# A two-layer hybrid decoder trunk: normalisations without GpSimd products, a power and one Newton step for the root, a new order at the first stage and the layer boundary, and compression interleaved with projections

## The chip, the cores and the metric

The kernel runs on one core of a Trainium2 chip. The metric is the time of one execution in microseconds on the device. The engines are named as in the profile: PE is the matrix engine, with its weight loads listed apart as PEld, DVE the vector engine, ACT the scalar engine, POOL the GpSimd engine, and SP the queue that issues every DMA of this kernel. Each engine works through its own list of instructions in order.

## The reference

The input x has 512 tokens of 1024 float32 channels. Two layers follow one another, each of this form:

```python
h = rms_norm(x, norm_g[l])              # x * rsqrt(mean(x*x) + 1e-6) * g
proj = h @ w_in[l]                      # 1024 -> 4376
...
y_nsa = nsa_attention(q, k_c, v_c, k_s, v_s, k_w, v_w, gates, ...)   # three branches
y_lru = rg_lru(u_lru, ...)              # short convolution, two gates, linear scan
y_conv = conformer_conv(glu_a, glu_b, ...)   # GLU, 31 taps per channel, LayerNorm, 512x512
mixed = concat([y_nsa * silu(z_nsa), y_lru * silu(z_lru), y_conv * silu(z_conv)])
x = x + mixed @ w_out[l]                # 1536 -> 1024
```

A last rms_norm with final_g closes the trunk. In the attention, one branch works on compressed keys and values: blocks of 32 tokens (31 of them, 16 apart) go through a small two-layer network, `silu(blk @ w1) @ w2`, with a 2048 x 256 matrix w1, once for keys and once for values.

## The kernel before

Every float32 product of matrices is made of three matmuls on split operands: a number is cast to the shorter type of the matrix engine (hi), and the rest, number minus hi, is the low part (lo); hi·hi, hi·lo and lo·hi are summed. So each weight tile needs a cast on ACT (line 146) and a subtraction on DVE (line 149, `lower`). x is held as four blocks of 128 tokens, t = 0 to 3, and the normalised input h as H, transposed: channels on partitions, tokens along the row, hi and lo.

Buffers come from pools with tags. Tag p has ten buffers of 1024 elements per partition, tag t sixteen of 512, "raw" two for weights as loaded, whi and wlo three each for split weights. PSUM has three buffers of tag ps, two each of tr and acc, and one of po. A tile waits until an earlier tile of its tag is free. The order of an engine's instructions is set by a scheduler from the order in the program, except where the program fixes it (`manual_schedule`): ACT and DVE in the first stage by the string START, PE in the last rows of the attention by LAST_ROWS.

The stages of a layer, in program order:

1. Normalisation. For a block: sum of squares on ACT (lines 221 and 296), the reciprocal root on DVE (`rsqrt`, line 208: a first guess from the bits of the number and three Newton steps, seven instructions on one element per partition), and the product with root and gain g. In layer 0 two blocks have the whole product on DVE (`product`, line 302) or in two parts, x times g on POOL (line 306) and times the root on ACT (line 309). In layer 1 and at the end (`rms_norm`, line 227) x times g is on POOL (line 232) and times the root on ACT (line 239); for the block t = 0 one half is on DVE (line 237). The gain is loaded as a broadcast to all partitions, 512 KB (`load_g`).
2. `turned` (line 273): eight transposes of a block on PE, a cast on ACT (line 278) and a lower on DVE (line 279) make its part of H.
3. The value projection (line 333): for each block 24 matmuls with 280 columns. Its weights are split by `value_weights` in eight pieces of 280 columns (casts on ACT, subtractions on POOL, or in START's v steps on DVE), held in sixteen buffers of tag t. In both layers the blocks go in the order 3, 2, 1, 0.
4. Channel parameters (lines 347 to 358): small loads into a buffer of tag t, transposed on PE.
5. The other projections (line 204, `proj`): for each tile of 128 output channels 24 matmuls with 512 columns, in the order glu, q, k_c and v_c, k, u_lru, z_nsa, z_lru, z_conv. In layer 0 the tables for the rotation are computed ahead of them on DVE. Between them stand the 31-tap filter on DVE (line 387, 120 instructions a layer), the scan, and the compression: `do_prep(c)` builds its operands, `do_main(c)` (line 617) loads w1 in two halves, splits each into two tiles and makes 64 matmuls of 256 columns (line 631). Keys (c = 0) come after z_nsa, values (c = 1) after z_lru.
6. LayerNorm of the convolution (`do_ln`, which calls `rsqrt`), part of the output projection (line 429, added to x on line 431), the 512x512 matmul (line 719), and the attention (lines 780 to 830).
7. `last_rows`: the attention's block 0, woven by LAST_ROWS with the output projection of its own part. Steps r are the rows of x: r31 is block 3, half 1. The last ones are r21, r31, r11, r01, r00. The output weights of half 1 are split into four buffers of tag p ("ow").

In layer 1, stage 1 also writes x back to memory (line 318), to be loaded again for the output projection.

## Time and profile before

| what | value |
|---|---|
| median of 3 runs | 809.26 us (807.87 to 812.53) |
| the profiled execution's own time | 808.92 us |
| its span, first to last instruction | 807.2 us |
| mean granted clock of PE | 0.985 |
| ACT busy | 462.8 us |
| POOL busy, instructions | 121.0 us, 184 |
| loads and stores | 82.53 MB, 102 GB/s in the mean |

The page gives busy time per engine, the span in 40 slices of 20.2 us each (each digit the busy share of one slice in tenths), the chain of waits that ended last, and groups of instructions. "Waits" name the instruction that came last before an engine went on. A matmul's duration in the records covers its whole way through the array, so matmuls overlap: the time of a group is better read from its first to its last start.

### The profile page before, as it was taken

To read this page: it belongs to the slowest core of one execution; us is meant where nothing else is said; L and a number is where in the kernel's file an instruction comes from. 1 tells how busy PE (TensorE), PEld (TensorE's weight loads), DVE (VectorE), ACT (ScalarE), POOL (GpSimd) and SP (SyncE) were. 2 spreads that over 40 slices of the span, in tenths; PEclk is the share of its full clock that TensorE was granted. 3 is DMA by queue.
4 is the path that set the end of the run, shared out by engine and by line. 5 is a ranking of instruction groups with operands and counts; after the bars stand their busy time and mean duration, and the time that the engine had idled before them with its cause. 6 is when DMAs were issued, how large, how long until landed. Compare 5 with 4: busy or idle time off the path is not lost.

```text
span 807.2 us, 11053 instructions
## 1 busy us (share of the span) xinstructions
PE 756.8 (94%) x3812; PEld 609.9 (76%) x3812; DVE 692.9 (86%) x1308; ACT 462.8 (57%) x908; POOL 121.0 (15%) x184
## 2 busy tenths in 40 slices
PE   3899999998999999999889999999899999999992
PEld 3778888687788786887777888776787878778872
DVE  6679999999998888878783899999999878888867
ACT  5434577684446566765562247669543466676654
POOL 4000000000000134343610000000000003333324
PEclk9999999999999999999979999999999999999997
DMA  5522375717542200102422225771664140010002
GB/s 190 164 80 86 105 185 128 186 59 240 201 147 79 78 1 2 53 2 58 157 95 94 97 64 153 183 179 37 202 231 157 52 158 1 1 54 1 2 27 104
DMA packets 68387, 82.53 MB, mean 102 GB/s; under 512 B 6616, under 2 KB 56856, under 8 KB 68332
## 3 DMA queue, kind: packets, MB, share of 16 engines
q1 hardware_dynamic: 68332, 81.83, 33.0%
q8 instruction: 30, 0.49, 0.3%
q14 instruction: 25, 0.20, 0.1%
HBM read 68.19 MB, written 4.19 MB: 90 GB/s over the span
## 4 chain that ended last, share of the span: by engine, by line
PE 60%; DVE 25%; ACT 6%; issue 4%; DMA 3%; POOL 2%; SPq 0%; DVEq 0%; POOLq 0%; ACTq 0%
PE acc L204 29%; PE acc L429 11%; DVE cv L387 6%; PE po L814 4%; DVE wlo L149 4%; PE pt L799 3%; PE acc L719 3%; ACT P L788 2%; PE acc L333 2%; PE ps L780 2%; PE ps L781 2%; DVE nw L214 2%; DVE xc L506 2%; POOL P L792 1%; DVE ss L215 1%
## 5 line engine op out<-in xcount | busy, mean ns | idle before, releaser
L204 PE MATMUL acc<-H,whi 128*128 128x512 f32 x1024 | 327.1, 399 | 0.6 <-ACT whi L146 0.6
L204 PEld LDWEIGHTS acc<-H,whi 128*128 128x128 f32 x1024 | 192.7, 189 | 47.8 <-issue 3.1
L204 PE MATMUL acc<-H,wlo 128*128 128x512 f32 x512 | 204.4, 400 | 0.3 <-DVE wlo L149 0.3
L146 ACT CAST whi<-raw 128x1024 fp32r<-128x1024 f32 x100 | 104.7, 1049 | 167.4 <-PE acc L204 126.7
L792 POOL TENSOR_SCALAR P<-P,hm,gt 128x384 f32<-128x384 f32 (+3 forms) x128 | 80.8, 640 | 593.9 <-DVE hm L790 586.0
L387 DVE SCALAR_TENSOR_TENSOR cv<-sg,dww,cv 128x496 f32<-128x496 f32 (+27 forms) x240 | 167.4, 742 | 0.9
L149 DVE TENSOR_TENSOR wlo<-raw,whi 128x1024 fp32r<-128x1024 f32 x100 | 123.7, 1237 | 25.0 <-ACT whi L146 24.6
L204 PEld LDWEIGHTS acc<-H,wlo 128*128 128x128 f32 x512 | 96.8, 189 | 24.0 <-issue 1.2
L788 ACT ACTIVATE P<-ps,hm 128x384 f32<-128x384 f32 (+3 forms) x128 | 67.0, 531 | 19.2 <-DVE hm L785 17.4
L802 DVE TENSOR_TENSOR pt<-pt 128x512 fp32r<-128x512 f32 (+1 forms) x88 | 54.4, 638 | 12.4 <-ACT pt L801 11.4
L785 DVE TENSOR_REDUCE hm<-ps 128x1 f32<-128x384 f32 (+3 forms) x88 | 55.2, 634 | 8.5 <-PE ps L782 6.0
L801 ACT CAST pt<-pt 128x512 fp32r<-128x512 f32 (+1 forms) x88 | 45.9, 548 | 24.2 <-PE pt L799 20.2
L814 PE MATMUL po<-pt,vv 128*128 128x256 f32 (+1 forms) x304 | 56.7, 303 | 0.4
L814 PEld LDWEIGHTS po<-pt,vv 128*128 128x128 f32 x304 | 44.4, 189 | 9.4 <-ACT pt L801 4.5
L799 PE MATMUL pt<-ident,P 128*128 128x128 f32 x320 | 47.7, 275 | 1.3 <-POOL P L792 0.6
L780 PE MATMUL ps<-KH,QS 128*128 128x384 f32 (+3 forms) x128 | 44.8, 362 | 1.4 <-ACT P L788 1.2
L799 PEld LDWEIGHTS pt<-ident,P 128*128 128x128 f32 x320 | 37.0, 140 | 6.5 <-POOL P L792 3.9
L781 PE MATMUL ps<-KL,QS 128*128 128x384 f32 (+3 forms) x128 | 40.7, 329 | 0.0
L431 DVE TENSOR_TENSOR x<-x,acc 128x512 f32<-128x512 f32 x48 | 32.7, 681 | 1.7 <-PE acc L429 1.3
L333 PE MATMUL acc<-wvh,H 128*128 128x280 f32 x128 | 29.4, 323 | 1.7 <-ACT H L278 1.7
L395 ACT COPY rs<-ru 32x512 f32<-32x512 f32 x48 | 29.7, 619 | 0.8
L276 PE MATMUL pt<-ident,hnat 128*128 128x128 f32 x64 | 13.4, 360 | 17.1 <-DVE hnat L303 8.6
(238 smaller groups left out, 1281.0 us busy)
## 6 DMA issues: line engine op xcount, KB each, us to landing
raw<-in_w_in_dram SPq DMA_DIRECT2D x30, 1024.0 KB
raw<-in_w_out_dram SPq DMA_DIRECT2D x12, 1024.0 KB
raw<-in_cmp_w_dram SPq DMA_DIRECT2D x8, 1024.0 KB
x<-in_x_dram SPq DMA_DIRECT2D x8, 512.0 KB
raw<-in_w_in_dram SPq DMA_DIRECT2D x4, 512.0 KB
QS<-rs SPq DMA_DIRECT2D x8, 256.0 KB
QS<-ru SPq DMA_DIRECT2D x8, 256.0 KB
KH<-rs SPq DMA_DIRECT2D x8, 256.0 KB
```

The costliest lines, as they stand in the source:

```text
L146: S.copy(out, in_)
L149: (eng or V).tensor_tensor(out, in_, hi.bitcast(F32), op=OP.subtract)
L204: PE.matmul(p, w[k], h[k], start=n == 0, stop=n == 23)
L387: V.scalar_tensor_tensor(a[:, s:], u[:, :T - s], dww[:, ct, j:j + 1], a[:, s:], op0=OP.mult, op1=OP.add)
L429: PE.matmul(p, h[:, k], w, start=m == 0, stop=m == 11)
L780: PE.matmul(sc[:, r, :], q, KH[g][:, b, :L], start=r == 0, stop=False)
L781: PE.matmul(sc[:, r, :], q, KL[g][:, b, :L], start=False, stop=False)
L785: V.tensor_reduce(hm[:, 0, :nh], sc, axis=AX.X, op=OP.min)
L788: S.activation(P[:, r * L:(r + 1) * L], sc[:, r, :], AF.Exp, scale=-1.0, bias=hm[:, 0, r:r + 1], accum_out=hm[:, 1, r:r + 1])
L792: G.tensor_scalar(P[:, r * L:(r + 1) * L], P[:, r * L:(r + 1) * L], hm[:, 2, r:r + 1], GA[i][:, h0 + r, 1 + b:2 + b], op0=OP.mult, op1=OP. ...
L799: PE.transpose(pt[:, kb, :], P[:, kb * 128:(kb + 1) * 128], ident)
L814: PE.matmul(po, v, PT[w][:, kb].rearrange("p r q -> p (r q)"), start=False, stop=last and kb == i and w == 1)
```

## The change

Five things are changed.

The root: `rsqrt` takes four times the mean square and raises it to the power -0.5 on POOL, which gives half the root wanted, and makes one Newton step on DVE with three short instructions. All its callers pass 4 where they passed 0.5.

The products: none is left on POOL. `rms_norm` makes one DVE instruction of x, root and gain (two halves for t = 0).

The first stage: layer 0's gain is loaded as one row and spread over the partitions by two matmuls with a row of ones, into two PSUM buffers of tag ps, from which the products on DVE read. The value weights' load stands ahead of x's blocks 1 and 0. START is rewritten; products are by halves, and the value weights are split in three pieces (3, 3 and 2 rows of 128 channels), all lowers on DVE, into the buffers of KH, KL and QS instead of tag t.

The boundary: layer 1's value weights are split ahead of the normalisation, the blocks go in the order 2, 3, 1, 0 (also at the end), and only two of the four "ow" tiles are taken from tag p, the others from whi and wlo.

The compression: `do_main` is given a generator of projections and makes two projection tiles ahead of each half of w1; z_nsa is woven into the keys' compression and z_lru into the values'. The values' `do_prep` comes ahead of the keys' `do_main`.

```diff
-START = "q3 c3 p3 q2 g2 q1 c2 t30 t31 s2 w2 c1 q0 p1 w0 c0 w1 t20 w3 t21 p0 v4 t10 v7 t01 t00 v5 v6 t11"
+START = "q3 c3 p30 p31 q2 t30 c2 t31 p20 w0 p21 q1 t20 c1 w1 t21 p10 q0 p11 w2 t10 c0 t11 p00 p01 t00 t01"
...
+    G.memset(one, 1.0)
+    power = const.tile([128, 1], F32, name="power")
+    G.memset(power, -0.5)
...
-    def rsqrt(y, hv):
-        s = work.tile([128, 1], F32, name="nw", tag="nw", bufs=4)
-        V.tensor_scalar(y.bitcast(I32), hv.bitcast(I32), -0.5, float(0x5f3759df - 2 ** 22 - 2 ** 31), op0=OP.mult,
-                        op1=OP.add)
-        for _ in range(3):
-            V.scalar_tensor_tensor(s, y, hv, y, op0=OP.mult, op1=OP.mult)
-            V.scalar_tensor_tensor(y, s, 1.5, y, op0=OP.subtract, op1=OP.mult)
+    def rsqrt(y, v4):
+        s = work.tile([128, 2], F32, name="nw", tag="nw", bufs=4)
+        G.tensor_tensor(y, v4, power, op=OP.pow)
+        V.tensor_scalar(s[:, 0:1], v4, -1.0, None, op0=OP.mult)
+        V.scalar_tensor_tensor(s[:, 1:2], y, s[:, 0:1], y, op0=OP.mult, op1=OP.mult)
+        V.scalar_tensor_tensor(y, s[:, 1:2], 3.0, y, op0=OP.add, op1=OP.mult)
...
-    def rms_norm(x, gb, name, last=False):
-        y = pair(name)
-        ss = rms_sums(x, y)
-        for n in range(1 if last else 2):
-            G.tensor_tensor(y[:, n], x[:, n], gb[:, n], op=OP.mult)
...
+        for n in (slice(0, 1), slice(1, 2)) if halves else (slice(0, 2),):
+            V.scalar_tensor_tensor(y[:, n], x[:, n], ss[:, 2:3], gb[:, n], op0=OP.mult, op1=OP.mult)
         return y
...
         if l == 0:
-            load_x(0, X, (3,))
-        gb = load_g(norm_g[l])
+            grow = pair("grow")[0:1].rearrange("p a c -> p (a c)")
+            SP.dma_start(out=grow, in_=norm_g[0:1, :])
+            load_x(0, X, (3, 2))
+        else:
+            gb = load_g(norm_g[l])
+        wv = [w_cols(l, (COL["v_s"], 128), (COL["v_w"], 152), rows=rows) for rows in ((0, 6), (6, 2))]
         if l == 0:
-            load_x(0, X, (2, 1, 0))
-        wv = [w_cols(l, (COL["v_s"], 128), (COL["v_w"], 152), rows=(k, 4)) for k in (0, 4)]
+            load_x(0, X, (1, 0))
...
-        def value_weights(k, eng=G):
-            src = wv[k // 4][:, k % 4, :]
-            hi = big(f"wvh{k}", F32R)[:, :280]
-            lo = big(f"wvl{k}", F32R)[:, :280]
+        def value_weights(j):
+            n = 3 if j < 2 else 2
+            src = wv[j // 2][:, 3 * j % 6:3 * j % 6 + n, :]
+            hi, lo = (main.tile([128, 4 if j == 2 else 2, 512], F32R, name="wv",
+                                tag=(f"kh{j}", f"kl{j}")[w] if j < 2 else f"qs{w}", bufs=1) for w in range(2))
...
+            gp = [psum.tile([128, 512], F32, name="acc", tag="ps", bufs=3) for n in range(2)]
+            for n in range(2):
+                PE.matmul(gp[n], one, grow[:, n * 512:(n + 1) * 512], start=True, stop=True)
...
-            def product(t):
-                V.scalar_tensor_tensor(hs[t], X[t], ss[t][:, 2:3], gb, op0=OP.mult, op1=OP.mult)
-            def gained(t):
-                G.tensor_tensor(hs[t], X[t], gb, op=OP.mult)
-            def scale(t):
-                S.activation(hs[t], hs[t], AF.Copy, scale=ss[t][:, 2:3])
+            def product(t, n):
+                V.scalar_tensor_tensor(hs[t][:, n], X[t][:, n], ss[t][:, 2:3], gp[n], op0=OP.mult, op1=OP.mult)
...
         else:
-            for t in (3, 2, 1, 0):
+            for j in range(3):
+                value_weights(j)
+            for t in (2, 3, 1, 0):
                 SP.dma_start(out=saved[t], in_=X[t])
-                h = rms_norm(X[t], gb, "hnat", last=t == 0)
+                h = rms_norm(X[t], gb, "hnat", t == 0)
                 for n in range(2):
                     turned(t, h, n)
-            for k in range(8):
-                value_weights(k)
...
-        for t in (3, 2, 1, 0):
+        for t in (2, 3, 1, 0) if l else (3, 2, 1, 0):
...
-                hi, lo = w_split(r[:, k:k + 2], [pair("ow", F32R) for _ in range(2)] if pairs else None)
+                hi, lo = w_split(r[:, k:k + 2], [pair("ow", F32R) for _ in range(2)] if pairs and k else None)
...
-        def do_main(c):
+        def do_main(c, between):
...
             for hf in range(2):
+                for _ in range(2):
+                    next(between)
                 r = raw_tile().rearrange("p (k c) -> p k c", c=256)
...
-        do_z_nsa()
-        do_main(0)
+        do_prep(1)
+        do_main(0, z_nsa())
         do_scan()
-        do_prep(1)
-        do_z_lru()
-        do_main(1)
+        do_main(1, z_lru())
...
-    for t in (3, 2, 1, 0):
-        o = rms_norm(X[t], gb, "o", last=t == 0)
+    for t in (2, 3, 1, 0):
+        o = rms_norm(X[t], gb, "o", t == 0)
```

The generators `z_nsa` and `z_lru` are the former `do_z_nsa` and `do_z_lru` with a `yield` behind each tile. In LayerNorm only the factor 0.5 becomes 4.

More of the change, by code (lines that the diff above doesn't have):

```diff
@@ L75, in tile_hybrid_trunk @@
     identb = const.tile([128, 128], BF16, name="identb")
-    zeros = big("zeros")[:, :192]
+    zeros, one = (lambda z: (z[:, :192], z[0:1, 384:]))(big("zeros"))
     ones = const.tile([128, 1], F32, name="ones")
@@ L279, in turned @@
             V.tensor_tensor(H2[1][n][:, :, sl], p, H2[0][n][:, :, sl].bitcast(F32), op=OP.subtract)
-        def value_weights(k, eng=G):
-            src = wv[k // 4][:, k % 4, :]
-            hi = big(f"wvh{k}", F32R)[:, :280]
-            lo = big(f"wvl{k}", F32R)[:, :280]
+        def value_weights(j):
[3 more added lines that the diff above has]
+                                tag=(f"kh{j}", f"kl{j}")[w] if j < 2 else f"qs{w}", bufs=1) for w in range(2))
+            hi, lo = (w.rearrange("p a b -> p (a b)")[:, :n * 280].rearrange("p (k c) -> p k c", k=n) for w in (hi, lo))
             cast(hi, src)
-            lower(lo, src, hi, eng)
-            WV[k] = (hi, lo)
+            lower(lo, src, hi)
+            WV[3 * j:3 * j + n] = [(hi[:, k], lo[:, k]) for k in range(n)]
         if l == 0:
             hs, ss = {}, {}
+            gp = [psum.tile([128, 512], F32, name="acc", tag="ps", bufs=3) for n in range(2)]
+            for n in range(2):
+                PE.matmul(gp[n], one, grow[:, n * 512:(n + 1) * 512], start=True, stop=True)
             def squares(t):
@@ L298, in chain @@
             def chain(t):
-                V.tensor_scalar(ss[t][:, 3:4], ss[t][:, 0:1], 0.5 / DM, 0.5 * EPS, op0=OP.mult, op1=OP.add)
+                V.tensor_scalar(ss[t][:, 3:4], ss[t][:, 0:1], 4.0 / DM, 4.0 * EPS, op0=OP.mult, op1=OP.add)
                 rsqrt(ss[t][:, 2:3], ss[t][:, 3:4])
-            def product(t):
-                V.scalar_tensor_tensor(hs[t], X[t], ss[t][:, 2:3], gb, op0=OP.mult, op1=OP.mult)
-            def gained(t):
-                G.tensor_tensor(hs[t], X[t], gb, op=OP.mult)
-            def scale(t):
-                S.activation(hs[t], hs[t], AF.Copy, scale=ss[t][:, 2:3])
-            steps = dict(q=squares, c=chain, p=product, g=gained, s=scale, t=lambda t, n: turned(t, hs[t], n),
-                         w=value_weights, v=lambda k: value_weights(k, V))
+            def product(t, n):
+                V.scalar_tensor_tensor(hs[t][:, n], X[t][:, n], ss[t][:, 2:3], gp[n], op0=OP.mult, op1=OP.mult)
+            steps = dict(q=squares, c=chain, p=product, t=lambda t, n: turned(t, hs[t], n), w=value_weights)
             with tc.manual_schedule(engines={mybir.EngineType.Activation, mybir.EngineType.DVE}):
@@ L581, in do_z_lru @@
                 ML32.append(HL[ct])
+                yield
         def do_z_conv():
@@ L680, in do_ln @@
                 V.bn_aggr(mv[:, 0:2], st)
-                V.tensor_scalar(mv[:, 1:2], mv[:, 1:2], 0.5, 0.5 * EPS, op0=OP.mult, op1=OP.add)
+                V.tensor_scalar(mv[:, 1:2], mv[:, 1:2], 4.0, 4.0 * EPS, op0=OP.mult, op1=OP.add)
                 rsqrt(mv[:, 2:3], mv[:, 1:2])
```

19 lines of the change are left out of this document (7 added, 12 removed).

## The prediction

> **What bounds the kernel now.** I read the page first (busy shares and the 40 slices), then a table of stretches, then the timeline and the chain of waits at the three places where the table shows TensorE (PE) idle.
>
> ```profile
> span 807.2 us, 11053 instructions
> PE 756.8 (94%) x3812; PEld 609.9 (76%) x3812; DVE 692.9 (86%) x1308; ACT 462.8 (57%) x908; POOL 121.0 (15%) x184
> PE   3899999998999999999889999999899999999992
> ```
>
> PE is busy nearly everywhere, so 807.2 - 756.8 = 50.4 us of idle PE is about all that reordering can win, with time at a reduced clock added. The slices put most of it at the start, at the layer boundary (slices 20 and 21) and at the end.
>
> ```profile
> 0.00:30.00 30.00, 16.73 (x90) 14.44 (x91) 22.36 (x53) 16.55 (x31) 9.07 (x22) 1.00 0.55 174
> 36.40:38.90 2.50, 0.76 (x7) 0.40 (x6) 0.52 (x2) 0.59 (x2) 0.00 (x0) 1.00 0.06 22
> 38.90:44.00 5.10, 5.10 (x17) 4.05 (x17) 0.55 (x3) 0.46 (x1) 0.00 (x0) 0.67 0.22 53
> 135.00:240.00 105.00, 101.97 (x457) 79.28 (x457) 103.74 (x145) 60.12 (x85) 0.00 (x0) 1.00 0.53 162
> 401.60:405.20 3.60, 0.00 (x0) 0.00 (x0) 3.50 (x10) 1.14 (x2) 2.15 (x2) 0.96 0.01 2
> 405.20:415.30 10.10, 8.11 (x35) 7.42 (x36) 9.42 (x28) 6.50 (x14) 3.32 (x3) 0.51 0.13 52
> 427.90:429.80 1.90, 0.44 (x5) 0.40 (x5) 0.52 (x2) 0.38 (x2) 0.73 (x2) 1.00 0.05 20
> 525.00:630.00 105.00, 102.12 (x456) 79.41 (x456) 101.42 (x141) 61.35 (x86) 0.00 (x0) 1.00 0.51 157
> 792.70:807.20 14.50, 0.00 (x0) 0.00 (x0) 10.00 (x34) 6.11 (x10) 3.91 (x4) 0.66 0.37 145
> ```
>
> The columns are the stretch, its length, then busy time of PE, weight load, VectorE (DVE), ScalarE (ACT), GpSimd (POOL), and the granted clock. PE idles 13.3 us in the first 30, 1.7 at 36.4, 3.6 at 401.6 (followed by 10 us at half clock), 1.5 at 427.9, 14.5 at the end, and 3.0 and 2.9 in the two middles. In those idle stretches at the boundary and the end DVE is the busy engine. The timeline of the end shows with what:
>
> ```profile
> 787.81 6.26 POOL L232 TENSOR_TENSOR o<-x,g 128x512 f32<-128x512 f32 x5 [7.67 <-ACT o L221]
> 790.42 1.21 DVE L215 SCALAR_TENSOR_TENSOR ss<-nw,ss 128x1 f32<-128x1 f32 x1
> 792.27 0.40 PE L429 MATMUL acc<-wlo,mn 128*128 128x512 f32 x1
> 794.37 0.16 DVE L215 SCALAR_TENSOR_TENSOR ss<-nw,ss 128x1 f32<-128x1 f32 x1
> 798.31 0.68 DVE L431 TENSOR_TENSOR x<-x,acc 128x512 f32<-128x512 f32 x1
> 802.28 0.22 DVE L214 SCALAR_TENSOR_TENSOR nw<-ss 128x1 f32<-128x1 f32 x1
> 802.80 0.75 DVE L237 SCALAR_TENSOR_TENSOR o<-x,ss,g 128x512 f32<-128x512 f32 x1
> ```
>
> A one-element DVE instruction that takes 0.16 us alone takes 1.21 us while POOL multiplies x by the gain. The root's seven dependent DVE instructions are stretched so, the queue is in order, and the residual add of the last row block, ready when PE ends at 792.67, starts at 798.31.
>
> **The end.** The change removes all POOL products and four of the root's seven DVE instructions, and two of the four "ow" buffers of tag p; ten exist, and before, x (4), zn (2) and ow (4) hold them all, so the squares cannot start before zn is read:
>
> ```profile
> 395.09 0.53 DVE L827 SCALAR_TENSOR_TENSOR m<-m,zn 128x256 f32<-128x256 f32 x1
> 395.96 0.63 ACT L221 ACTIVATE hnat<-x 128x512 f32<-128x512 f32 x1
> ```
>
> With the new order the blocks 2, 3 and 1 are normalised while PE still works. The last block: add 792.7 to 793.4 (0.68, row above), square 0.8 (0.63 plus an accumulator read), 0.15 for the sum, the power, Newton's two instructions (0.22 + 0.16, with gaps 0.45), two half products of 0.75. The power on POOL is an operation that the trace does not show. Its bounds:
>
> ```profile
> L90 POOL TENSOR_SCALAR_AFFINE_SELECT seen<-ones 128x1 f32<-128x1 f32 x1 | 0.2, 185 | 0.0
> L232 POOL TENSOR_TENSOR o<-x,g 128x512 f32<-128x512 f32 x7 | 8.8, 1282 | 12.2 <-ACT o L221 10.1 <-issue 2.1
> 386.99 0.18 DVE L790 RECIPROCAL hm<-hm 128x4 f32<-128x4 f32 x1 [1.57 <-ACT P L788]
> 387.35 1.73 POOL L792 TENSOR_SCALAR P<-P,hm,gt 128x128 f32<-128x128 f32 x4 [4.70 <-DVE hm L790]
> ```
>
> One element per partition costs POOL 0.19 us; 512 of them with two inputs cost 1.28. I take 0.4, near the first since the size is the same, with some for the heavier arithmetic, and 0.18 each way for the hand-over (387.35 less 387.17). So power and hand-overs are 0.75 (0.55 to 1.65). The whole root is 0.15 + 0.75 + 0.45 = 1.35 against about 1.5 undisturbed before (seven of 0.16 to 0.22 with their gaps): the gain is not a shorter root but an undisturbed one. The last product then ends at 793.4 + 0.8 + 1.35 + 1.5 = 797.0 instead of 803.55: 6.5 us (5 to 7.5).
>
> The rule against this stands in the Trainium skill, page SBUF — State Buffer, section Who interferes with whom: a GpSimd instruction that reads SBUF and a DVE instruction with two SBUF inputs exclude each other for the whole instruction, and the power reads SBUF as the products did. By it a power that meets a full-width product of two SBUF tensors waits up to that product; at one meeting per exposed block this would take about 1.3 us from the end and as much from the boundary, 2.6 in all; the 1.21 us row agrees with the rule.
>
> **The boundary.** PE ends the output projection at 401.6 and the input projections run gaplessly only from 429.8. The work between:
>
> ```profile
> 420.05 4.70 PE acc L333 x36
> 22.61 0.46 PE pt L276 x4
> 392.24 0.69 DVE L431 TENSOR_TENSOR x<-x,acc 128x512 f32<-128x512 f32 x1 [0.28 <-PE acc L429]
> 407.61 0.68 DVE L431 TENSOR_TENSOR x<-x,acc 128x512 f32<-128x512 f32 x1
> ```
>
> 96 value matmuls at 4.70/36 = 0.13 are 12.5 us, 32 transposes at 0.46 for four are 3.7, with 1 for changing between them 17.2 in all. Block 3 has its sum at 392.9, block 2 before it, and with p buffers free both are normalised before 401.6, so PE goes on with their transposes at once. The last block's residual add moves from 407.61 to about 401.7; its H is ready near 409 (add 0.7, square 0.8, root 1.35, and in the same DVE queue eight lowers of 0.68 and two half products), and the value matmuls of the other three cover that until about 414. Added on DVE: products of 1.28 for three blocks (ACT scaled before) and the value weights' lowers, 2.7 us that were on POOL; both lie before 401.6, under PE work, where DVE is busy 9.7 of 12.6 us. If that cover fails it costs 2 to 3 us here. Projections then run from about 401.6 + 17.2 + 1.2 (first transposes waiting for ACT and DVE) = 420.0, plus the parameter transposes of 0.4: 9.4 us sooner than 429.8. For one more collision on DVE I take 8.5 (6 to 10.5).
>
> In that is the wait for the channel parameters: their buffer is of tag t, all 16 of which the split value weights hold; the change puts these in kh, kl and qs, idle then, so the parameter loads leave SP's queue early and the 1.5 us hole goes.
>
> **The first stage.**
>
> ```profile
> 4.27 1.06 ACT L296 ACTIVATE hnat<-x 128x1024 f32<-128x1024 f32 x1 [2.19 <-DMA x<-in_x_dram]
> 9.38 2.04 DVE L214 SCALAR_TENSOR_TENSOR nw<-ss 128x1 f32<-128x1 f32 x1
> 25.95 1.23 DVE L149 TENSOR_TENSOR wlo<-raw,whi 128x1024 fp32r<-128x1024 f32 x1 [0.22 <-ACT whi L146]
> 27.09 0.45 DVE L149 TENSOR_TENSOR wvl<-raw,wvh 128x280 fp32r<-128x280 f32 x1
> 27.45 0.68 DVE L279 TENSOR_TENSOR H<-pt,H 128x512 fp32r<-128x512 f32 x1
> 30.39 3.35 PE acc L333 x27
> 33.74 4.70 DMA nat<-in_conv_dw_w_dram
> ```
>
> The gain's 512 KB broadcast becomes 4 KB and two matmuls from one row; the value weights' load moves ahead of x's blocks 1 and 0. SP issues the row first, so x's block 3 lands about 0.4 later, its sum stands at 5.9. After that DVE works in the order written by hand: four roots of 1.35 with the queue waiting on POOL (5.4), eight half products of 0.7 (5.6), eight lowers of 0.68 (5.4), three weight lowers scaled from 1.23 for 1024 columns (1.0, 1.0, 0.7). That is 19.1, so to 25.0, plus about 1.6 of waits for transposes, so the last H at 26.6, not 28.1. That alone is little. More comes from the weights. In DVE's order two thirds are split at 17.5 and the rest at 20, where before the last came at 27.5. So PE can do about 9 value matmuls early and, from 18 to 26.6 less 2.4 of transposes, 48 more at 0.13; before, 46 of 96 were still left at 30.4. Then 39 remain, 5 us, and projections begin at 31.6. Before, they ran from 38.9, less 2.6 us of them (eleven, between the value matmuls) done earlier, plus about 1.3 lost at clock 0.67 behind the hole at 36.4: in effect 37.6. Gain 6 (4 to 9).
>
> **The middle.** PE's own waits for compression weights:
>
> ```profile
>   DVE wlo L149: 11.7, 14
> 236.35 0.74 DVE L387 SCALAR_TENSOR_TENSOR cv<-sg,dww,cv 128x511 f32<-128x511 f32 x1
> 239.69 0.88 PE pt L676 x8
> ```
>
> Of the 11.7 us (matmul and weight load queues counted both, two layers) PE loses at most its 3.0 and 2.9. A compression weight tile costs DVE 1.23 and PE eight matmuls of 256 columns, 1.0 at the 0.13 of 280 columns; a projection tile 1.23 and 24 of 512 columns, 5.6. Alternating, two and two, gives three buffers time to fill. At each return to a projection a split of about 2.3 (the lower's 1.23 and a cast of the square's 1.06) stands against 2 us of compression matmuls, so about 0.4 remains four times: 1.5 us won per layer, 3 together (0 to 5.5). DVE is full there, and its filter taps end at 237, 2.6 us before PE needs them: it could swallow this gain, but the tables for the rotation, queued on SP behind the parameter loads before, now come while DVE waits for the first projections (busy 0.55 of 5.1 us at 38.9 before). Moving the second preparation ahead of the first compression puts its small loads in front of weight loads on SP; two raw buffers hold four projection tiles, 22 us of PE work, so I cost it nothing; uncovered it would be one small load, the 4.7 us of the parameters above.
>
> LayerNorm's eight roots lose four DVE instructions of 0.2 and gain hand-overs, under about 20 us of PE's output projection: nothing (1 either way).
>
> **Sum.** 6.5 + 8.5 + 6 + 3 = 24 us from the profiled execution's 808.92 (span 807.2 and 1.7 around it): 784.9; its time is 0.3 below the median of the runs. I say 785. The forecast's own range, all four terms at the ends and partly compensating, is 778 to 793.
>
> **Rivals.** (1) The stages stay bound by DVE: the hand-written order leaves DVE waiting at every root, and products and weight lowers now on DVE delay the H lowers. For it: DVE is busy 22.4 of the first 30 us and 9.4 of 10.1 at 405. Half of the first stage's and boundary's gains go: 785 + 7 = 792, to 800 with the power at its upper bound (0.9 more on eight exposed roots). (2) POOL fetches code for its first power while DVE's queue waits in the first root. Nothing in the trace shows one; POOL's first products come in at their usual length:
>
> ```profile
> 9.05 2.35 POOL L306 TENSOR_TENSOR hnat<-x,g 128x1024 f32<-128x1024 f32 x1 [5.75 <-ACT hnat L296]
> ```
>
> That is within two of the 1.28 us halves, so the fetch lies between nothing and some 5 us, the idle PE time still in front of the first value matmul: 785 to 790. The Trainium skill, GPSIMD Engine Reference, section Instruction dispatch, has the first call of a freshly loaded kernel cost about 6 us invisibly; by it the time would be 791, an estimate, and no row here shows it. (3) Slower: the power itself is long. It decides from (24 + 4)/8 = 3.5 us more per root, eight of them exposed (four in the first stage, two each at boundary and end): 813 and up. Against it: POOL's 1.28 us for 512 elements. (4) The middle's gain is not there and (1) holds too: 796 to 800; with a power of about 3 us no change, 805 to 813.
>
> **Chances.** Forecast 0.62, rival 1 0.18, rival 2 0.06, better than 778 (the upper ends of all terms) 0.06, rival 4's no change 0.04, rival 3 0.04. About half a per cent, 4 us, can be told from no change in this kernel: faster 0.92, same 0.04, slower 0.04. The range 776 to 800 leaves out no change, slower, and the far part of better: 0.12, and some of rival 1.
>
> **What would show it.** Right: no POOL product in the norm, one-element DVE instructions at 0.15 to 0.22 at boundary and end; PE restarting within 1.5 us of the output projection, clock near 1 there; projections gapless by about 31.6 and 18.5 us after the boundary; last product about 4.3 us after PE's last matmul; no wait for the channel parameters. Wrong: a power well over 1 us on POOL, PE idle over 3 us at the boundary, value matmuls waiting on weight lowers, or new waits of projections in the middle as long as those for compression were.

## The result, and the profile after

The changed kernel takes 785.79 us in the median of four runs (785.11 to 786.91), the kernel before beside it 810.58 (four runs, 807.87 to 812.53): a ratio of 0.9698, 95% interval 0.9664 to 0.9732. The profiled execution took 786.09 us, its span is 784.3. The forecast was 785.

First the page: span, busy time, and PE and its granted clock in 40 slices of 19.6 us.

```profile
span 784.3 us, 10943 instructions
PE 755.0 (96%) x3816; PEld 604.8 (77%) x3816; DVE 676.4 (86%) x1243; ACT 452.1 (58%) x889; POOL 101.7 (13%) x179
PE   6999999999999999999989999999999999999995
PEclk9999999999999999999999999999999999999998
```

PE's work is the same (755.0 us against 756.8); its idle time fell from 50.4 to 29.3 us. The 3 at the start has become a 6, the dip over two slices at the boundary one 8. The table of stretches (length, busy time of PE, weight load, DVE, ACT, POOL, granted clock) at the places that answer to those shown of before:

```profile
0.00:30.00 30.00, 23.28 (x126) 19.65 (x127) 19.23 (x48) 16.65 (x29) 5.11 (x23) 1.00 0.61 191
394.70:398.30 3.60, 1.46 (x12) 1.01 (x10) 3.60 (x5) 2.62 (x6) 0.00 (x0) 1.00 0.38 146
398.30:408.40 10.10, 9.92 (x80) 9.58 (x78) 8.03 (x20) 4.44 (x10) 1.49 (x3) 1.00 0.35 105
412.50:414.40 1.90, 1.90 (x18) 1.67 (x18) 0.47 (x2) 0.37 (x1) 0.00 (x0) 1.00 0.00 0
414.00:614.00 200.00, 197.47 (x869) 156.24 (x868) 185.87 (x273) 107.66 (x151) 0.00 (x0) 1.00 0.48 140
776.95:784.30 7.35, 0.00 (x0) 0.00 (x0) 2.95 (x8) 0.72 (x2) 0.55 (x1) 0.68 0.36 144
```

At the boundary PE works again at once, though with two waits (it is busy 1.46 of the first 3.6 us, before 0), the 10 us behind it have the clock 1.00 instead of 0.51 with 80 matmuls instead of 35, and the hole in front of the channel parameters (412.5 to 414.4) is gone. At the end 7.35 us are left of 14.5. The timeline there:

```profile
776.98 0.69 DVE L425 TENSOR_TENSOR x<-x,acc 128x512 f32<-128x512 f32 x1
777.70 0.63 ACT L225 ACTIVATE o<-x 128x512 f32<-128x512 f32 x1 [2.02 <-DVE x L425]
778.88 0.55 POOL L215 TENSOR_TENSOR ss<-ss,power 128x1 f32<-128x1 f32 x1 [3.93 <-DVE ss L228]
779.48 0.22 DVE L217 SCALAR_TENSOR_TENSOR nw<-ss,nw 128x1 f32<-128x1 f32 x1 [0.48 <-POOL ss L215]
779.73 0.16 DVE L218 SCALAR_TENSOR_TENSOR ss<-nw,ss 128x1 f32<-128x1 f32 x1
779.93 1.42 DVE L231 SCALAR_TENSOR_TENSOR o<-x,ss,g 128x512 f32<-128x512 f32 x2
```

The last residual add stands right behind the last matmul (before, 5.6 us later), and the one-element instructions take 0.22 and 0.16. The power takes 0.55, and the products end at 781.35, 4.4 us after PE.

To compare kernels, the span of each one's profiled execution is cut at five points of PE's timeline: the first LayerNorm transpose of each layer, the end of row r00 of each layer, and the end. The stretches are start to LayerNorm (first stage and middle of layer 0), LayerNorm to r00 in layer 0, boundary and middle of layer 1, LayerNorm to r00 in layer 1, and the tail.

| kernel | median us | ratio to before, 95% | span | start to LN | LN to r00 | boundary, middle | LN to r00 | tail |
|---|---|---|---|---|---|---|---|---|
| before | 810.58 | 1 | 807.2 | 239.5 | 162.1 | 229.4 | 161.7 | 14.5 |
| changed | 785.79 | 0.966 to 0.973 | 784.3 | 231.5 | 163.1 | 219.3 | 162.9 | 7.35 |
| 1 old root | 792.33 | 0.978 to 0.981 | 791.2 | 239.8 | 162.3 | 218.8 | 161.7 | 8.6 |
| 2 and POOL products | 804.15 | 0.993 to 0.996 | 803.6 | 239.9 | 164.8 | 220.8 | 169.3 | 8.85 |
| 3 old root in LayerNorm | 784.24 | 0.968 to 0.971 | 782.6 | 230.5 | 162.6 | 219.4 | 162.7 | 7.4 |
| 4 power twice | 795.44 | 0.982 to 0.985 | 794.6 | 232.7 | 166.0 | 222.0 | 165.9 | 8.1 |
| 5 no interleaving | 790.31 | 0.974 to 0.977 | 787.9 | 232.0 | 163.1 | 222.5 | 162.9 | 7.4 |
| 6 four ow from p | 789.55 | 0.973 to 0.976 | 787.6 | 231.8 | 163.7 | 220.1 | 162.5 | 9.6 |
| 7 late weights | 793.49 | 0.978 to 0.981 | 792.5 | 238.4 | 163.0 | 220.5 | 163.2 | 7.4 |
| 8 before, DVE products | 802.90 | 0.989 to 0.992 | 799.2 | 238.0 | 162.2 | 226.9 | 161.9 | 10.2 |
| 9 before, new root | 808.88 | 1.000 to 1.003 | 806.4 | 238.8 | 162.4 | 229.0 | 162.7 | 13.6 |
| 10 mixed roots | 783.20 | 0.967 to 0.970 | 782.5 | 231.7 | 162.2 | 218.8 | 162.4 | 7.35 |
| 11 early turns | 782.49 | 0.966 to 0.969 | 781.5 | 231.3 | 164.6 | 215.4 | 162.9 | 7.3 |
| 12 both | 784.89 | 0.970 to 0.975 | 783.1 | 231.0 | 167.3 | 215.0 | 162.5 | 7.4 |

Each ratio is to runs of the kernel before on the same chip (medians 808.28 to 810.58). From before to changed: 8.0 won in the first stage and middle, 10.0 in the boundary and middle, 7.2 in the tail, and 1.1 and 1.2 lost between LayerNorm and r00; together 22.9, as the spans have it.

### The profile page after: what moved, and what is told of

Read it like the earlier page. It is cut to its first block, busy times and chain, and to the rows that moved or that the text cites. A ratio compares the mean times of both kernels' runs of the same rounds, so it can differ in the third digit from the quotient of the medians.

```text
span 784.3 us, 10943 instructions
## 1 busy us (share of the span) xinstructions
PE 755.0 (96%) x3816; PEld 604.8 (77%) x3816; DVE 676.4 (86%) x1243; ACT 452.1 (58%) x889; POOL 101.7 (13%) x179
## 4 chain that ended last, share of the span: by engine, by line
PE 78%; DVE 9%; ACT 6%; issue 4%; POOL 2%; DMA 0%; POOLq 0%; DVEq 0%; SPq 0%; ACTq 0%
PE acc L208 43%; PE acc L423 10%; PE po L813 5%; PE pt L798 3%; PE acc L718 3%; PE acc L327 3%; PE ps L779 2%; ACT P L787 2%; PE ps L780 2%; DVE wlo L153 1%; DVE cv L381 1%; PE pt L630 1%; POOL P L791 1%; ACT pt L800 1%; PE pt L735 1%
## 5 line engine op out<-in xcount | busy, mean ns | idle before, releaser
L150 ACT CAST whi<-raw 128x1024 fp32r<-128x1024 f32 x102 | 106.5, 1050 | 159.4 <-PE acc L208 130.1
L381 DVE SCALAR_TENSOR_TENSOR cv<-sg,dww,cv 128x493 f32<-128x493 f32 (+18 forms) x240 | 165.9, 737 | 0.9
L208 PEld LDWEIGHTS acc<-H,wlo 128*128 128x128 f32 x512 | 96.2, 188 | 27.3 <-DVE wlo L153 3.4
L801 DVE TENSOR_TENSOR pt<-pt 128x512 fp32r<-128x512 f32 (+1 forms) x88 | 54.2, 638 | 12.9 <-ACT pt L800 11.8
L813 PE MATMUL po<-pt,vv 128*128 128x256 f32 (+1 forms) x304 | 58.0, 304 | 1.1 <-DVE pt L801 0.7
L215 POOL TENSOR_TENSOR mv<-mv,power 128x1 f32<-128x1 f32 x8 | 4.2, 544 | 418.1 <-DVE mv L680 418.1
L813 PEld LDWEIGHTS po<-pt,vv 128*128 128x128 f32 x304 | 44.7, 189 | 9.8 <-ACT pt L800 4.6
L327 PE MATMUL acc<-wv,H 128*128 128x280 f32 x192 | 30.6, 313 | 2.5 <-ACT wv L150 1.5
L423 PE MATMUL acc<-whi,mn 128*128 128x512 f32 x96 | 31.1, 406 | 0.0
```

The costliest lines, as they stand in the source:

```text
L150: S.copy(out, in_)
L208: PE.matmul(p, w[k], h[k], start=n == 0, stop=n == 23)
L381: V.scalar_tensor_tensor(a[:, s:], u[:, :T - s], dww[:, ct, j:j + 1], a[:, s:], op0=OP.mult, op1=OP.add)
L423: PE.matmul(p, h[:, k], w, start=m == 0, stop=m == 11)
L813: PE.matmul(po, v, PT[w][:, kb].rearrange("p r q -> p (r q)"), start=False, stop=last and kb == i and w == 1)
```

## Experiments: root or products

**1. The old root everywhere.**

```diff
-        G.tensor_tensor(y, v4, power, op=OP.pow)
-        V.tensor_scalar(s[:, 0:1], v4, -1.0, None, op0=OP.mult)
-        V.scalar_tensor_tensor(s[:, 1:2], y, s[:, 0:1], y, op0=OP.mult, op1=OP.mult)
-        V.scalar_tensor_tensor(y, s[:, 1:2], 3.0, y, op0=OP.add, op1=OP.mult)
+        V.tensor_scalar(y.bitcast(I32), hv.bitcast(I32), -0.5, float(0x5f3759df - 2 ** 22 - 2 ** 31), op0=OP.mult,
+                        op1=OP.add)
+        for _ in range(3):
+            V.scalar_tensor_tensor(s, y, hv, y, op0=OP.mult, op1=OP.mult)
+            V.scalar_tensor_tensor(y, s, 1.5, y, op0=OP.subtract, op1=OP.mult)
```

> The changed kernel with the old root everywhere (a guess from the bits and three Newton steps, seven DVE instructions, no power on POOL); products stay on DVE. Theory A, that the gain at boundary and end comes from taking the products off POOL and not from a shorter root: an undisturbed old root takes about 1.5 us against 1.23 for power and one step, so some 0.3 us on each of eight exposed roots, 2 us, and about 2 us won back in the LayerNorm stage where the power is the slower one; span 784 (782 to 787), and 4.4 to 5.0 us from the last matmul to the end of the last product. Rival B, that the root carries the gain: 6 us or more come back, span 790 and more, and one-element DVE instructions over 1 us are seen again.

Measured: span 791.2, in size as rival B has it, but without its sign: no one-element instruction is stretched. Behind the first stage and middle (8.2 us longer) the old root is 1.3 us shorter in all: 0.8, 0.5 and 1.3 won, 1.25 lost in the tail. The timeline of DVE and PE in the first stage shows what went wrong there:

```profile
19.19 0.43 DVE L126 CAST ang<-pi 128x512 f32<-128x512 int32 x1 [2.74 <-DMA pi<-in_positions_dram]
19.53 0.15 DVE L215 TENSOR_SCALAR ss<-ss 128x1 int32<-128x1 int32 x1
19.65 0.48 DVE L127 TENSOR_SCALAR ang<-ang,inv 128x512 f32<-128x512 f32 x1
22.71 1.02 DVE L153 TENSOR_TENSOR wv<-raw,wv 128x840 fp32r<-128x840 f32 x1
23.79 2.94 PE L328 MATMUL acc<-wv,H 128*128 128x280 f32 x11 [3.92 <-DVE wv L153]
```

The hand-written order fixes only its own steps. The scheduler put instructions of the rotation tables into the gaps of the seven dependent ones, the first of them in front of the third root, where DVE's queue stood 2.74 us until the positions landed. The weights behind it came 6 us later (22.71 against 16.60), and PE ran into half clock. So the root is not what won, but in the first stage it decides what slips in between.

**2. The same with POOL products at boundary and end.**

```diff
-        for n in (slice(0, 1), slice(1, 2)) if halves else (slice(0, 2),):
-            V.scalar_tensor_tensor(y[:, n], x[:, n], ss[:, 2:3], gb[:, n], op0=OP.mult, op1=OP.mult)
+        for n in range(1 if halves else 2):
+            G.tensor_tensor(y[:, n], x[:, n], gb[:, n], op=OP.mult)
...
+            S.activation(y, y, AF.Copy, scale=rstd)
```

The products stand ahead of the root; for the block t = 0 one half is on DVE, as before the change.

> The first experiment's kernel (old root) with x times gain on POOL and the scaling on ACT again in the normalisation of the boundary and the end, as before the change; the first stage, the order of the blocks and the buffers stay as changed. Theory A: one-element DVE instructions beside a POOL product take over 1 us again, 4.5 us from last matmul to last product becomes 9 to 11, the boundary from the last matmul to the gapless projections goes from 19.4 to 23 to 27; 8 to 12 us above the first experiment, span 792 to 797. Rival C, that block order, free buffers and early value weights made the boundary and the end short: at most 3 us above the first experiment.

Measured: 12.4 us of span above the first experiment, as theory A had it, but at another place: the tail grew by 0.25 only, the stretch before it by 7.7. The timeline and PE's waits of the last 100 us:

```profile
775.39 3.95 POOL L231 TENSOR_TENSOR o<-x,g 128x512 f32<-128x512 f32 x3 [1.14 <-ACT o L226]
775.63 1.33 DVE L836 TENSOR_TENSOR mn<-m,mn 128x256 fp32r<-128x256 f32 x1
776.89 1.24 DVE L218 SCALAR_TENSOR_TENSOR nw<-ss 128x1 f32<-128x1 f32 x1
778.17 1.18 DVE L219 SCALAR_TENSOR_TENSOR ss<-nw,ss 128x1 f32<-128x1 f32 x1
```

```profile
PE po L820 <- DVE pt L808: 2.6, 1, 2.6
PE acc L430 <- DVE mn L836: 0.8, 1, 0.8
PE acc L430 <- DVE x L432: 0.7, 1, 0.7
```

```profile
780.13:786.96 6.83, 6.50 (x15) 4.65 (x16) 5.03 (x16) 3.68 (x6) 1.27 (x1) 0.50 0.23 95
```

Three DVE instructions that take 0.42, 0.22 and 0.16 alone take 1.33, 1.24 and 1.18 beside the POOL products: each ends about when one of them does. This bears out, with these rows, the Trainium skill's rule on the page SBUF — State Buffer, section Who interferes with whom, that such instructions shut each other out for their whole length. With early buffers the POOL products fall among the last attention rows, and PE waits for DVE there instead of at the end. The three waits listed are 4.1 us of the 7.7; behind the first one the clock is at half for 6.83 us, with 6.50 us of PE work in that time, which is some 3.3 more.

**3 and 4. The power in the LayerNorm, and twice everywhere.**

```diff
-                rsqrt(mv[:, 2:3], mv[:, 1:2])
+                rsqrt_old(mv[:, 2:3], mv[:, 1:2])
```

> The changed kernel with the old root in the LayerNorm only (eight roots of 28). If the power there is what lost 1.1 us a layer between the first LayerNorm transpose and the end of the output projection: that stretch goes from 163.15 and 162.94 back to about 162.0, the wait of PE for ACT's normalised tile (0.58) goes, span 782.2 (781.5 to 783). Rival, that the loss is from the matmuls and transposes falling in another order because the stage starts with other queues: no change, 784.3 within 0.7.

```diff
-        G.tensor_tensor(y, v4, power, op=OP.pow)
+        for o in (s[:, 1:2], y):
+            G.tensor_tensor(o, v4, power, op=OP.pow)
```

> The changed kernel with every power made twice on POOL, one after the other, the first one's result unused: each root 0.54 us longer and nothing else changed. By the prediction's count eight roots are exposed (four in the first stage, two each at boundary and end): 4.3 us, and 1 to 2 more in the two LayerNorms, span 789 to 791. Rival, that DVE's other work fills these waits and only the last root of the kernel is exposed: 0.5 to 1.5 us, span 785 to 786.

The third gave back 0.6 and 0.2 us of the 1.1 and 1.2, and PE's wait for ACT there went; 1.0 us more came from the first stage, where nothing was changed (below, on the clock). The fourth fell on neither side: 10.3 us, not 4.3 to 6 and not 1. PE's waits in it, and the stretch behind r00:

```profile
PE pt L692 <- ACT nt L685: 3.0, 2, 1.5
PE pt L676 <- ACT nt L685: 2.1, 2, 1.1
```

```profile
402.66:408.66 6.00, 6.00 (x31) 5.98 (x30) 4.04 (x10) 1.71 (x3) 2.00 (x4) 0.53 0.58 175
```

In each LayerNorm PE now waits 2.55 us (5.1 in the two layers) where it waited 0.6. At the boundary a little more waiting brought the half clock (0.53 over 6 us); with about 6 us of PE work in that spell it costs some 3 us, so the 2.7 us lost in that stretch are the clock's. The first stage lost 1.2, the tail 0.7, and the two stretches from LayerNorm to r00 2.8 and 2.9. The three places with roots counted as exposed thus lost 4.6 us with the clock, close to the 4.3 expected though split otherwise; what falls is the 1 to 2 us for the LayerNorms, whose eight roots lost 5.7, 0.71 each for a power of 0.54. Over all 20 roots (the expectation of the third counts 28) it is 0.51 each. The profiled execution is the slowest of the four: the others took 793.84 to 796.04 at mean clocks of 0.998 to 0.996, this one 796.35 at 0.993, so without the half clock the doubled power costs up to 2.5 us less.

**8 and 9. One part alone in the kernel before.** Eight, the products on DVE, with the old root, order, buffers and first stage:

```diff
-        for n in range(1 if last else 2):
-            G.tensor_tensor(y[:, n], x[:, n], gb[:, n], op=OP.mult)
...
+        for n in (slice(0, 1), slice(1, 2)) if last else (slice(0, 2),):
+            V.scalar_tensor_tensor(y[:, n], x[:, n], ss[:, 2:3], gb[:, n], op0=OP.mult, op1=OP.mult)
```

Nine, the new root alone (the first experiment's diff the other way round), with POOL's and ACT's products as before.

> The kernel before with one part of the change alone: in the normalisation of the boundary and the end the product of x, root and gain is one DVE instruction (two halves for the last block), nothing on POOL and no scaling on ACT; old root, old block order, all four ow buffers, old first stage and middle. If the POOL products are what made boundary and end long whatever the rest: tail 14.5 to 9 to 11 and the boundary 28.1 to 23 to 25, 7 to 10 us less, span 797 to 800. If the products alone do little because the squares wait for buffers and the last block's chain stays behind the others in DVE's queue: 0 to 4 us less, span 803 to 807.

> The kernel before with the new root alone (power on POOL, one Newton step on DVE), the products and scalings on POOL and ACT as before. Theory A, that the products and the buffers carry the gain: nothing won, since three stretched DVE instructions replace seven, but each power stands in POOL's queue behind products of 1.28 us: the end 14.5 within 1.5, the boundary within 2, LayerNorm 0.5 to 1 a layer worse; span 805 to 811. Rival B, that the shorter root is a gain of its own: four stretched instructions of 1.2 us less on the exposed roots, 4 to 5 us at the end and as much at the boundary, span 797 to 800.

The products alone won 8.0 us of span: 4.3 in the tail, 2.4 at the boundary, and 1.5 ahead of the first LayerNorm, which the edit does not touch (the clock from 38 to 44 us is 1.00 here and 0.72 in the kernel before). So 6.5 us are the products' own. The profiled execution is the fastest of its four (800.89, the others 802.83 to 803.01); by the medians the edit won 7.35. The root alone won nothing, and its rows in the tail show why:

```profile
790.48 0.55 POOL L213 TENSOR_TENSOR ss<-ss,power 128x1 f32<-128x1 f32 x1
791.07 1.24 DVE L215 SCALAR_TENSOR_TENSOR nw<-ss,nw 128x1 f32<-128x1 f32 x1 [1.59 <-POOL ss L213]
792.34 1.20 DVE L216 SCALAR_TENSOR_TENSOR ss<-nw,ss 128x1 f32<-128x1 f32 x1
```

The power waited behind a product in POOL's queue, DVE waited 1.59 for it, and the two Newton instructions were stretched by the next product. Rival B falls.

## Experiments: buffers, weights, interleaving

**6. Four ow tiles from tag p.**

```diff
-                hi, lo = w_split(r[:, k:k + 2], [pair("ow", F32R) for _ in range(2)] if pairs and k else None)
+                hi, lo = w_split(r[:, k:k + 2], [pair("ow", F32R) for _ in range(2)] if pairs else None)
```

> The changed kernel with all four split tiles of the last output weights from tag p again, as before the change. Theory: x, zn and ow hold all ten buffers, so the first square at boundary and end starts about 8 us later, when zn is read, and three normalisations of some 3 us of DVE each run past the end of the output projection: boundary 19.4 to 22 to 24, tail (last matmul to end) 7.35 to 8 to 10, together 3 to 8 us, span 787 to 792. Rival, that the freed buffers cover nothing because DVE's work sets the pace: within 1 us of 784.3.

Measured: 3.3 us, 2.3 of them in the tail. The first square of the end starts at 772.32, 5.7 us before r00 ends at 777.98, and the other normalisations come so late that two of their products still stand in DVE's queue around that end, the first of them ahead of the last add, which comes at 779.90:

```profile
772.32 0.63 ACT L225 ACTIVATE o<-x 128x512 f32<-128x512 f32 x1
778.70 1.28 DVE L231 SCALAR_TENSOR_TENSOR o<-x,ss,g 128x1024 f32<-128x1024 f32 x1
779.90 0.68 DVE L425 TENSOR_TENSOR x<-x,acc 128x512 f32<-128x512 f32 x1
```

At the boundary it is 0.8, with 0.5 before it. The theory's lower end.

**7. The value weights late in the first stage.**

```diff
-START = "q3 c3 p30 p31 q2 t30 c2 t31 p20 w0 p21 q1 t20 c1 w1 t21 p10 q0 p11 w2 t10 c0 t11 p00 p01 t00 t01"
+START = "q3 c3 p30 p31 q2 t30 c2 t31 p20 p21 q1 t20 c1 t21 p10 q0 p11 w0 t10 c0 t11 p00 w1 p01 t00 t01 w2"
```

> The changed kernel with the three splits of the value weights late in the first stage's hand-written order (the last one as the last step), all else the same. The prediction's theory, that most of the first stage's gain comes from the early weights: the matmuls of the value projection that now fill the time from 16 to 25 us run after 26, two accumulators can wait for the last piece and the rest cannot start, so projections begin at 35 to 38 rather than 31.5, span 788 to 791. Rival, that the chain of H (roots, products, lowers) sets the start: at most 1.5 us, span 784 to 786.

Measured: projections begin at 36.7, not 31.5. Only 48 of the 96 value matmuls stand before 30.4:

```profile
30.45 6.46 PE L327 MATMUL acc<-wv,H 128*128 128x280 f32 x48 [0.72 <-DVE gt L335]
36.74 0.63 PE L208 MATMUL acc<-H,whi 128*128 128x512 f32 x2
```

The rival falls: the last H lower ends at 27.3 here, before the 27.9 of the changed kernel, and the start is 5.2 later. The first full clock is also later here (22.46 us against 18.47, below), which is an uncounted part of the 5.2. Two other stretches of this kernel are longer by 1.7 and 1.1 from the clock alone (below).

**5. No interleaving.** `do_main` makes no projections, and the sequence is the old one:

```diff
-        do_prep(1)
-        do_main(0, z_nsa())
+        for _ in z_nsa():
+            pass
+        do_main(0)
         do_scan()
-        do_main(1, z_lru())
+        do_prep(1)
+        for _ in z_lru():
+            pass
+        do_main(1)
```

> The changed kernel with the old sequence in the middle: z_nsa's four tiles, then the keys' compression, the scan, the second preparation, z_lru's four tiles, then the values' compression. The prediction's theory: the interleaving is worth 1.5 us a layer; from the first gapless projection to the first LayerNorm transpose it takes 200.0 us in both layers now and would take 201.5 (201.2 to 202), span 787 (786.5 to 788.5). Rival, that the middle got shorter for another reason (the tables and the second preparation moved, DVE freed): at most 0.3 us a layer, span 784 to 785.

Measured: 1.35 us more in layer 0's middle and 2.1 in layer 1's (1.0 of the boundary's 3.2 is the clock again). The size is the prediction's, the reason is not. PE's waits for compression weights, first the changed kernel's in layer 1, then this one's, and this one's timeline and stretches there:

```profile
PE pt L630 <- DVE wlo L153: 1.5, 1, 1.5
PE acc L208 <- DVE wlo L153: 1.0, 1, 1.0
```

```profile
PE pt L628 <- DVE wlo L153: 2.2, 2, 1.7
PE acc L208 <- DVE wlo L153: 0.2, 1, 0.2
```

```profile
561.36 0.38 PE L628 MATMUL pt<-wlo,cMs 128*124 128x256 f32 x1 [1.72 <-DVE wlo L153]
563.10 0.57 PE L628 MATMUL pt<-wlo,cMs 128*124 128x256 f32 x1 [0.53 <-DVE wlo L153]
```

```profile
560.00:564.00 4.00, 2.11 (x12) 1.90 (x13) 4.00 (x6) 1.04 (x1) 0.00 (x0) 0.85 0.55 191
564.00:568.00 4.00, 4.00 (x20) 3.31 (x19) 3.31 (x5) 1.59 (x3) 0.00 (x0) 0.72 0.98 302
```

The listed waits are 2.5 and 2.4 us: interleaving did not shorten them. It moved them apart, and without it the two waits of 1.72 and 0.53 cost clock behind them in layer 1: 4 us at 0.85 and 4 at 0.72 are 1.7 us of full clock. Waits of the same size in layer 0 cost none. A smaller part is PE's wait for ACT's copy behind each compression: 1.6 us over four here (in the weight load queue), none in the changed kernel, where projections stand in between. How the 1.35 of layer 0, which lost no clock, divide was not settled further.

## Experiments: a better version

**10. The old root in LayerNorm and boundary, the power in the first stage and at the end.**

```diff
-                h = rms_norm(X[t], gb, "hnat", t == 0)
+                h = rms_norm(X[t], gb, "hnat", t == 0, 0.5)
...
-                rsqrt(mv[:, 2:3], mv[:, 1:2])
+                rsqrt_old(mv[:, 2:3], mv[:, 1:2])
```

The 0.5 makes `rms_norm` call the old root.

> The changed kernel with the old root in the LayerNorm and at the layer boundary; the power stays in the first stage and in the final normalisation. From the stretches of the first and third experiments: the stretch from the first LayerNorm transpose to the end of the output projection 162.3 in layer 0 and 162.7 in layer 1 (163.1 and 162.9 in the changed kernel), the boundary 18.8 to 19.4, the rest as changed: span 782 to 783.5. If the power costs DVE nothing there that the seven instructions of the old root do not cost too: 784.3 within 0.7.

**11. Blocks 2 and 3 turned inside the last rows.** In the changed kernel's profile PE waits at the boundary for its first H, though block 2's product is ready at 384.2: its transposes stand behind r00 in PE's order. The edit issues layer 1's loads, weight splits and norms within `last_rows`:

```diff
-LAST_ROWS = "s10 c s00 r30 s01 r20 d r10 t00 o0 t01 s11 v00 v01 r21 t10 t11 r31 o1 v10 v11 r11 r01 r00"
+EARLY_ROWS = "s10 c s00 r30 s01 r20 d r10 t00 o0 t01 s11 v00 v01 r21 t10 t11 r31 o1 v10 v11 w n2 r11 h20 h21 n3 r01 h30 h31 r00"
```

Step w is the loads and splits, n the normalisation of a block, h the eight transposes in two halves; layer 1 ends with the old LAST_ROWS.

> The changed kernel with the boundary started earlier: the loads and splits of layer 1's value weights and the normalisation of block 2 are issued inside the last rows, with the transposes of block 2 on PE behind the row r11 and those of block 3 behind r01, instead of behind r00. In the changed kernel PE waits 0.89 and 1.25 us there for the first H, and in two of the runs so far the clock falls to 0.73 to 0.78 for the next 6 us (1.1 us more). If these waits are only a matter of PE's order: boundary 19.4 less the 8 to 16 transposes now made earlier (0.9 to 1.9) and less 2.1 of waits, 15.4 to 17.5, and the stretch before it longer by the transposes; span 781.5 to 783. If DVE, which is busy all the time from 394 to 401, is what H waits for: no gain, 784 to 786, the waits only move.

**12. Both.**

> Both of the last two edits in the changed kernel: blocks 2 and 3 turned inside the last rows, and the old root in the LayerNorm and at the layer boundary. If they act in different places, their gains add: 1.8 us of span from the root and 2.8 from the early turns, 784.3 less 4.6 = 779.7 (779 to 781), and against the changed kernel's 785.8 a time of about 781. If both win the same time, DVE's queue around the boundary: 781 to 782.5 of span.

Ten won 1.8 us of span at the stretches named. Eleven won 2.8: the boundary to the gapless projections is 15.5 instead of 19.4, the stretch before it 1.4 longer by the transposes. Its five runs (782.31 to 783.24) all lie below the four of the changed kernel; the two were not run side by side, and against the kernel before the ratio is 0.9673 (0.966 to 0.969), which the interval of the changed kernel (0.966 to 0.973) contains. The two do not add: twelve is 1.6 us of span slower than eleven. Its timeline:

```profile
392.99 1.28 DVE L242 SCALAR_TENSOR_TENSOR hnat<-x,ss,g 128x1024 f32<-128x1024 f32 x1
394.42 1.06 PE L295 MATMUL pt<-ident,hnat 128*128 128x128 f32 x8 [3.27 <-DVE nw L220]
```

The old root's instructions were strewn among other DVE work, block 3's product ended at 394.2 instead of 389.6, and PE, whose order is fixed there, held r00 for 3.27 us (the row names the one-element instruction that starts beside the product's end). The shortest median is experiment 11's.

## Why the prediction was right, and where not

**The end**: 6.5 forecast, 7.2 measured; the last product 4.4 us after PE, 4.3 forecast. The mechanism holds with its two parts: undoing the buffers costs 2.3 in the tail, the products alone won 4.3. What the prediction did not see is that POOL's products with free buffers would stretch the attention before the end (experiment 2): in the kernel before, the late squares had kept them out of it.

**The boundary**: 8.5 forecast, 8.8 measured (28.1 us from r00 to gapless projections, now 19.4). The 8.5 means 19.6; the 18.5 named as a sign leaves out the 0.4 for the parameters and the 0.9 for one more collision that the 8.5 counts. The parts tried alone give less: 2.4 for the products, 0.8 for the buffers. The sum assumed full clock, and that needs PE to wait little: before, 10 us at 0.51 with 8.1 us of PE work cost about 4 us. Order of blocks and early weights at the boundary were not undone separately, so their share is argued, not shown.

**The first stage**: 6 forecast, 6.1 measured; projections from 31.5, forecast 31.6. Early weights carry it, as said: 5.2 us by experiment 7. The last H came at 27.9, not 26.6. About 1.5 of the 6.1 is the half clock behind the hole at 36.4, which the prediction took at 1.3; experiment 8's execution of the same first stage did not have it, so this part is not won in every execution.

**The middle**: 3 forecast, 3.2 between the two profiles (1.9 and 1.25), 3.45 by experiment 5. The step that failed is "about 0.4 remains four times" (its own rows, 2.3 against two tiles of eight matmuls at 0.13, leave 0.2): the waits were 2.6 in layer 0 and 2.5 in layer 1, one of 1.5 and one of about 1 a layer; the listed waits of the kernel without interleaving are no longer. The gain came in part from the spacing of the waits, which in experiment 5 was worth 1.7 us of clock in layer 1 and none in layer 0, and in part from PE's work behind the compression; that the size was met is luck. (A compression has 32 matmuls of 256 columns; the 64 named ahead of the prediction are those of a layer.)

**LayerNorm**: "nothing (1 either way)" failed. 1.1 and 1.2 us were lost from LayerNorm to r00. Its roots lie under less of PE's output projection than the 20 us forecast: in layer 0 some 38 of its matmuls, about 9 us, stand between the first transpose and the first one of a normalised tile, where the kernel before has 50. PE waited 0.58 for ACT's tile behind them, and in layer 1 0.7 more in the attention for a lower (L813 for L801), a wait that is absent with the old root everywhere. The old root in LayerNorm alone gave back 0.8 of 2.3, everywhere 2.1. These waits are not the whole account: PE's idle time in the two stretches is 3.75 and 4.05 us against 3.96 and 3.87 before, while its busy time grew by 1.3 and 1.0. What slows PE there is open.

**The power**: 0.4 forecast, 0.55 measured, within its bounds; the root at the start took 1.23 us, 1.35 forecast. That only eight roots are exposed failed: doubling the power cost the LayerNorms' eight, which the prediction puts at nothing, more than the others (5.7 of 10.3 us in experiment 4). If the loss grew in proportion, a power at 1.28, near its upper bound, would by an estimate from experiment 4 have cost 0.73 / 0.54 x 10.3 = 14 us more, about twice what rival 1 allowed; that the sum held is owed to a power near the low end of its bounds.

**The rivals**: 2 falls, the first power (6.17, 0.55) is as short as the last, which also answers the 6 us of the Trainium skill's page GPSIMD Engine Reference, section Instruction dispatch: for this operation no run here shows them. 3 falls with 0.55 us. 1 and 4 did not come about at boundary and start.

So the total was right to 1 us, with 2.3 us lost in LayerNorm and attention where none was forecast, against surpluses of 0.7, 0.3, 0.1 and 0.2 in the other four terms. That these nearly cancel is luck.

## To carry to other kernels

Look at what an instruction of another engine does to DVE's whole queue before counting how many instructions a step has: taking products off POOL won 6.5 us in the kernel before and 12.4 in the changed one (with the clock behind the waits), a shorter root alone none. A short wait on another engine inside an in-order queue can be paid where it was counted as hidden, so double it once and see at each stage, rather than count which are exposed. Waits of PE that add to about 2 us within some 3.4 us can be paid twice, by the clock behind them: spread them, or put ready work between them. And before a microsecond is put down to an edit, see whether the clock differs in a stretch that the edit does not touch.

## What the runs showed of the hardware that was not expected

**The clock.** At the boundary the changed kernel and experiment 7 have the same PE order and almost the same waits, and the clock differs. First the changed kernel's PE timeline, then experiment 7's:

```profile
396.23 0.40 PE L327 MATMUL acc<-wv,H 128*128 128x280 f32 x1 [0.89 <-ACT H L273]
397.88 0.66 PE L271 MATMUL pt<-ident,hnat 128*128 128x128 f32 x4 [1.25 <-DVE H L274]
```

```profile
403.02 0.40 PE L327 MATMUL acc<-wv,H 128*128 128x280 f32 x1 [0.89 <-ACT H L273]
404.70 1.10 PE L271 MATMUL pt<-ident,hnat 128*128 128x128 f32 x4 [1.28 <-DVE H L274]
```

Waits of 0.89 and 1.25 left the clock at 1.00; 0.89 and 1.28 brought it to half and cost 1.1 us. The sum of the waits hardly differs, but their place does. The traces keep the granted clock as spells. Before the last matmul, the 14 profiles have 13 spells at half clock; each is 3.41, 6.83 or 10.24 us long, and in each execution all spells begin and end on one grid with steps of 3.41 us. Where the grid lies differs from execution to execution. Here are two of its steps at these waits, first in the changed kernel, then in experiment 7:

```profile
393.94:397.35 3.41, 1.79 (x11) 1.17 (x9) 3.34 (x6) 3.38 (x8) 0.00 (x0) 1.00 0.13 53
397.35:400.76 3.41, 2.88 (x24) 2.88 (x25) 3.41 (x7) 1.17 (x2) 0.00 (x0) 1.00 0.98 291
```

```profile
401.34:404.75 3.41, 1.24 (x9) 0.79 (x7) 3.41 (x5) 2.79 (x7) 0.00 (x0) 1.00 0.31 124
404.75:408.17 3.42, 3.42 (x16) 3.41 (x17) 2.77 (x5) 1.17 (x2) 0.00 (x0) 0.50 0.96 286
```

In the changed kernel an edge of the grid falls into the second wait: 1.62 us of idle PE lie in one step and 0.53 in the next. In experiment 7 one step holds 2.17, and the next is at half clock. In layer 0's middle of experiment 7 one wait of 2.45, 2.02 of it within a step, did the same from 172.65 to 176.06. Over the 14 profiles each of the 13 spells began behind a step with 1.74 to 3.31 us of idle PE. Behind a full step with up to 1.71 none began, and two steps with 1.74 (experiment 6) and 1.82 (experiment 8) went without. So by these runs the edge is near half a step, and for waits of about 2 us the place of the grid decides. The Trainium skill, page TensorE: Matmul & The Clock Gate, section HAM oscillation — how this bites in real kernels, asks for no idle gaps of PE over about 3.4 us; by these runs much shorter ones are enough. It also means that the changed kernel's boundary, with its two waits, can lose 1.1 us in one execution and nothing in the next. That its four runs have mean clocks of 0.995 to 0.999 would fit, but only one of them left a trace.

**The first full clock.** In the first stage the same 24 value matmuls took 4.33 us in the changed kernel and 3.44 in experiment 3, which changes nothing there. What follows them starts 0.96 us earlier, and this is the 1.0 us of its table row, an effect of one execution and not of the edit:

```profile
16.25 4.33 PE L327 MATMUL acc<-wv,H 128*128 128x280 f32 x24
```

```profile
16.18 3.44 PE L336 MATMUL acc<-wv,H 128*128 128x280 f32 x24
```

The trace's clock records begin at 18.47 us in the changed kernel and at 16.36 in experiment 3. Before them the tables list 1.00 for want of a record, but these matmuls start 0.23 us apart up to that time and 0.13 behind it. In the 14 profiles the records begin between 16.36 and 22.46 us, so a single profile's first stage can differ by a microsecond or more without any edit.
